# Gate products of a transformer block: seven products for 11 of 32 weight pairs, and new distances of x1's transposes

## The chip, the core and the metric

The kernel runs on one core of a Trainium2 chip, in one launch. The metric is the device time of one execution in microseconds (us). The core's engines work at the same time, each through its own queue of instructions in order: PE (TensorE) multiplies matrices and transposes, DVE (VectorE) and ACT (ScalarE) work on elements, POOL (GpSimd) does a few steps and some transfers, SP (SyncE) issues most transfers. An instruction waits until what it reads is there and what it overwrites is no longer needed. PE writes its sums into eight PSUM banks of 128 x 512 fp32.

## What is computed

One block of a transformer on 256 tokens of width 2048, in fp32. A wide product of the input gives the operands of two branches and two gates. Branch a is a gated delta rule over 8 heads, branch b a sparse attention over 8 heads. Each branch is multiplied by its own weights and by the sigmoid of its gate; their sum goes through an output product, a residual sum with a layer norm, and an FFN of width 5632 with a second residual sum and layer norm. The lines that bear on the change:

```python
proj = x @ w_in[l]
(qkv_a, a_in, b_in, z, q_b, k_b, v_b, q_i, k_i, w_i, gate_a, gate_b) = jnp.split(proj, offsets, axis=-1)
...
merged = jax.nn.sigmoid(gate_a) * (o_a @ w_branch_a[l]) + jax.nn.sigmoid(gate_b) * (o_b @ w_branch_b[l])
x = layer_norm(DEEPNORM_ALPHA * x + merged @ w_out[l], ln1_g[l], ln1_b[l])

h_gate, h_up = jnp.split(x @ w_ffn_in[l], 2, axis=-1)
x = layer_norm(DEEPNORM_ALPHA * x + (jax.nn.silu(h_gate) * h_up) @ w_ffn_out[l], ln2_g[l], ln2_b[l])
```

Each gate is a product of 256 x 2048 with 2048 x 2048.

## The kernel before

Every fp32 operand is split into two parts of a shorter type (fp32r): `hi` is a cast on ACT, `lo` is the rest, a subtraction on DVE. A product is three matmuls into one bank: hi by hi, hi by lo, lo by hi. The input's parts are `XH` and `XL` (four tiles `X_0_85` to `X_3_88` in the profile and its order, hi and lo under one name); 256 tokens are two blocks of 128, `tb` 0 and 1.

Weights stream from HBM in chunks of 512 KB, 128 x 1024. `chunk` (L75 to 79) issues the load into `raw` on SP, the cast to `hi` on ACT (L77) and the subtraction to `lo` on DVE (L79), 70 places ahead of their turn; `raw`, `hi` and `lo` have a few buffers each, so how far this runs ahead of PE is set by PE's giving `hi` free, four chunks back.

PE's and SP's orders are written by hand, in the order of the program text. ACT's and DVE's come from priorities: a step of a chunk counts as 70 places earlier than it stands. After each chunk the code calls `tick()`; it counts a clock and lets the waiting chains (generators that were put in with `start`) issue their next step. A chain says how many ticks, or which event, it waits for, so that the attention, the delta rule and the layer norms are laced into the stream of matmuls. `need` only asserts that an event has been.

The gates: `gate(dst)` runs four blocks of 512 columns. `block_xs` takes two banks from `acc` (one for each `tb`) and goes through eight chunks; a chunk holds two k tiles of 128 rows by 512 columns, and `xs_mm` (L159 to 161) makes 12 matmuls of 512 columns from it. The sigmoid is taken from the bank by ACT. A gate has 384 matmuls. First comes gate b (`gb`, in `s_vT` and `s_t`), then the product of branch b with its weights, multiplied into `gb` (L833), then gate a (`ga`, in `s_kT` and `s_qT`), and branch a's product (L842, L843). During gate a the delta rule's output is gated (L765), transposed on PE into `aux` (L772) and split into `oh` and `ol` (L192, L193).

The FFN's output product already has pairs by seven products: a pair is two k tiles by 1024 columns, 24 matmuls in the plain way. With the scheme of Strassen and Winograd it takes seven block products in place of eight, 21 matmuls, on sums of weight blocks (`wt`, L1045 to 1049, split into `thi` and `tlo`, L1036 and L1038) and on combinations of the activations. Four of the seven products go to four banks of their own (`wbank`), which all such pairs of a group share, and which are combined once per group. `WQ` lists which pairs these are: 11 and 8 of 22.

x1's transposes: after the first residual sum, `ln` normalises each token block in four parts of 512 columns (L890, then L895) on DVE. `x1T_chain` puts PE's transposes of these parts (L808) between the last chunks of the output product and the first of the FFN; `X1T_WAIT = (4, 5)` are the ticks until the first, and `1 + tb` those between them. A tick there stands for six matmuls of 512 columns.

Of the kernel before, what the change touches and what calls it, by code (L numbers as in the profile page):

```python
# [34 lines left out]
X1T_WAIT = (4, 5)  # L35
# [14 lines left out]
def block_kernel(ctx: ExitStack, tc: tile.TileContext, xT, x, cpack, onehot, relb, convw, alog, dtb, gnw,  # L50
                 ws, wws, win, wba, wbb, wo, wfi, wfg, wfo, ln1g, ln1b, ln2g, ln2b, out):
# [944 lines left out]


    def pair_chunks(g, q, pool=None):
        return [chunk(wfo[g, 2 * q + i], pool) for i in range(2)]

    def mm3(o, xh, xl, hi, lo, first, last):
        nc.tensor.matmul(o, xh, hi, start=first, stop=False)  # L1002
        nc.tensor.matmul(o, xh, lo, start=False, stop=False)  # L1003
        nc.tensor.matmul(o, xl, hi, start=False, stop=last)  # L1004

    def plain(bank, cks, q, j, n, tb):

        k = 2 * q + (j + n) % 2
        ts = slice(tb * P, tb * P + P)
        hi, lo = cks[j]  # L1010
        cs = slice(n * 512, (n + 1) * 512)
        mm3(bank[2 * tb + n], hh_[:, k, ts], hl_[:, k, ts], hi[:, cs], lo[:, cs],
            q == 0 and j == 0, q == FT // 2 - 1 and j == 1)

    def plain_pair(bank, g, q):
        cks = pair_chunks(g, q)
        for j in range(2):
            for n in range(2):
                for tb in range(NTB):
                    plain(bank, cks, q, j, n, tb)  # L1020
            tick()

    def seven_pair(bank, wbank, g, q):
# [2 lines left out]
        with tc.high_priority(offset=LEAD):
            ra = wq.tile([P, 1024], F32, name="wraw", tag="wraw")
            nc.sync.dma_start(ra, wfo[g, 2 * q])
            rb = wp.tile([P, 1024], F32, name="raw", tag="raw")
            nc.sync.dma_start(rb, wfo[g, 2 * q + 1])  # L1030
            nc.sync.dma_start(gt.rearrange("p a b t -> p (a b t)").bitcast(F32), d_g[WALL.index(q)])

            def parts(src, tag, pool, bufs):
                n = src.shape[1]
                hi = pool.tile([P, n], F32R, name=tag + "hi", tag=tag + "hi", bufs=bufs)
                nc.scalar.copy(hi, src)  # L1036
                lo = pool.tile([P, n], F32R, name=tag + "lo", tag=tag + "lo", bufs=bufs)
                nc.vector.tensor_sub(lo, src, hi.bitcast(F32))  # L1038
                return [(hi[:, i:i + 512], lo[:, i:i + 512]) for i in range(0, n, 512)]

            b11, b22 = parts(ra, "", wp, None)
            b21, = parts(rb[:, :512], "", wp, None)
            b12 = rb[:, 512:]
            t13 = wq.tile([P, 1024], F32, name="wt", tag="wt")
            nc.vector.tensor_tensor(t13.rearrange("p (a n) -> p a n", a=2), ra.rearrange("p (a n) -> p a n", a=2),  # L1045
                                    bc(b12[:, None, :], [P, 2, 512]), op=OP.add)
            t24 = wq.tile([P, 1024], F32, name="wt", tag="wt")
            nc.vector.tensor_add(t24[:, :512], t13[:, :512], ra[:, 512:])
            nc.vector.tensor_add(t24[:, 512:], t24[:, :512], rb[:, :512])  # L1049
            t1, t3 = parts(t13, "t", wq, 3)  # L1050
            t2, t4 = parts(t24, "t", wq, 3)
        ka, kb = 2 * q, 2 * q + 1
        t0, t1s = slice(0, P), slice(P, S)
        first, last = q == WQ[g][0], q == WQ[g][-1]
        mm3(wbank[0], hh_[:, ka, t0], hl_[:, ka, t0], *b11, first, last)
        mm3(bank[1], gt[:, 0, 3], gt[:, 1, 3], *b22, False, False)
        mm3(bank[0], hh_[:, kb, t0], hl_[:, kb, t0], *b21, False, False)
        tick()
        mm3(wbank[3], gt[:, 0, 0], gt[:, 1, 0], *t1, first, last)
        mm3(wbank[2], gt[:, 0, 2], gt[:, 1, 2], *t3, first, last)  # L1060
        mm3(wbank[1], gt[:, 0, 1], gt[:, 1, 1], *t2, first, last)
        mm3(bank[2], hh_[:, kb, t1s], hl_[:, kb, t1s], *t4, False, False)
        tick()
# [37 lines left out]
    def group(g, ps_std, ps_w, n):  # L1101
        bank = [ps_std() for _ in range(4)]
        wbank = [ps_w() for _ in range(4)]
        for q in range(n):
            if g and q in LN2_LOAD:
                ln2_load(LN2_LOAD.index(q))
            if q in WQ[g]:
                seven_pair(bank, wbank, g, q)
# [4 lines left out]
        return bank
# [154 lines left out]
```

## Time and profile before

| | us |
|---|---|
| three runs | 1496.25, 1495.33, 1495.77 |
| median | 1495.77 |
| profiled execution | 1495.64 |
| its span in the trace | 1493.7 |
| gate b on PE | 406.2 to 493.2 |
| branch b's product | 493.2 to 536.7 |
| gate a on PE | 536.7 to 625.6 |
| branch a's product | 625.6 to 672.0 |

The span is the time from the first to the last instruction in the trace; 1.94 us of the execution lie around it. Times in rows of the trace count from its start. A row of the timeline gives start, duration, engine, line, operation, output and inputs, shape and count; in square brackets the idle time of the engine before it. A row of the groups gives the count, then the busy time and the mean in ns of one, then the idle time ahead of them and what ended it. Durations of matmuls overlap: a matmul of 512 columns shows as 0.39 us, so distances of starts are what counts.

### The profile page before, as it was taken

What the parts mean: (1) busy time and instruction counts of PE and PEld (TensorE: products, weight loads), DVE (VectorE), ACT (ScalarE), POOL (GpSimd) and SP (SyncE); (2) the same over time, 40 slices, a digit from 0 to 9 for tenths busy, and PEclk for the clock granted to TensorE, in tenths of its full rate; (3) what the DMA queues carried; (4) which work ended last, traced back from release to release, by engine and by line L of the source; (5) the groups of instructions that cost most, each with busy time, mean ns of one, the idle gap of its engine ahead of it and who ended that gap; (6) DMA issues with size and microseconds to landing.
All of it is one profiled execution on the core that took longest, in us unless ns stands there. A gap on an engine that the chain in (4) does not pass through costs nothing.

```text
span 1493.7 us, 20700 instructions
## 1 busy us (share of the span) xinstructions
PE 1478.3 (99%) x7863; PEld 1264.3 (85%) x7863; DVE 1010.2 (68%) x1434; ACT 734.4 (49%) x971; POOL 50.4 (3%) x59
## 2 busy tenths in 40 slices
PE   9999999999999999999999999999999999999997
PEld 9888888888888888888878888888888888888885
DVE  5798985466464554475675666666666666999986
ACT  5765443445444444444444545545455455554651
POOL 0011010020010000000000000000000000000000
PEclk9999999999999999999999999999999999999999
DMA  8646574434455655558636666666666566786862
GB/s 290 197 155 195 180 200 143 156 128 169 164 190 195 196 185 191 192 182 297 237 113 197 205 219 211 210 213 216 207 214 217 189 218 222 282 276 236 326 221 91
DMA packets 91828, 303.49 MB, mean 203 GB/s; under 512 B 16385, under 2 KB 17449, under 8 KB 91217
## 3 DMA queue, kind: packets, MB, share of 16 engines
q1 hardware_dynamic: 80592, 283.36, 56.6%
q0 software_dynamic: 4096, 16.45, 3.3%
q10 hardware_dynamic: 7040, 2.36, 0.7%
q8 instruction: 62, 1.02, 0.3%
q14 instruction: 38, 0.30, 0.1%
HBM read 290.40 MB, written 11.73 MB: 202 GB/s over the span
## 4 chain that ended last, share of the span: by engine, by line
PE 97%; DMA 1%; DVE 1%; ACT 0%; issue 0%; SPq 0%; POOLq 0%; DVEq 0%; ACTq 0%
PE acc L139 31%; PE acc L142 15%; PE acc L161 10%; PE acc L160 10%; PE acc L159 10%; PE acc L1003 3%; PE acc L1002 3%; PE acc L1004 3%; PE aux L1003 2%; PE aux L1002 2%; PE aux L1004 2%; DMA raw<-in_win_dram 1%; PE aux L593 1%; PE aux L808 0%; PE aux L747 0%; PE aux L487 0%
## 5 line engine op out<-in xcount | busy, mean ns | idle before, releaser
L79 DVE TENSOR_TENSOR lo<-raw,hi 128x1024 fp32r<-128x1024 f32 (+1 forms) x477 | 585.0, 1230 | 401.4 <-ACT hi L77 400.1
L77 ACT CAST hi<-raw 128x1024 fp32r<-128x1024 f32 (+1 forms) x477 | 496.8, 1044 | 572.9 <-PE acc L161 225.9
L139 PE MATMUL acc<-X,hi 128*128 128x512 f32 x1984 | 625.8, 397 | 0.0
L142 PEld LDWEIGHTS acc<-X,lo 128*128 128x128 f32 x1984 | 372.7, 188 | 88.0
L142 PE MATMUL acc<-X,lo 128*128 128x256 f32 x1984 | 390.0, 278 | 0.0
L139 PEld LDWEIGHTS acc<-X,hi 128*128 128x128 f32 x1984 | 302.1, 189 | 2.1 <-ACT hi L77 0.7
L159 PE MATMUL acc<-hi,X 128*128 128x512 f32 x544 | 214.3, 394 | 0.0
L161 PE MATMUL acc<-hi,X 128*128 128x512 f32 x544 | 211.9, 390 | 0.0
L160 PE MATMUL acc<-lo,X 128*128 128x512 f32 x544 | 211.8, 389 | 0.0
L161 PEld LDWEIGHTS acc<-hi,X 128*128 128x128 f32 x544 | 102.1, 188 | 21.3
L160 PEld LDWEIGHTS acc<-lo,X 128*128 128x128 f32 x544 | 102.2, 188 | 20.6
L159 PEld LDWEIGHTS acc<-hi,X 128*128 128x128 f32 x544 | 102.2, 188 | 20.4
L1036 ACT CAST thi<-wt 128x1024 fp32r<-128x1024 f32 x38 | 40.0, 1053 | 40.4 <-DVE wt L1049 22.4
L1002 PE MATMUL acc<-hi,hH 128*128 128x512 f32 x131 | 51.0, 389 | 0.0
L1003 PE MATMUL acc<-lo,hH 128*128 128x512 f32 x131 | 51.0, 389 | 0.0
L1004 PE MATMUL acc<-hi,hL 128*128 128x512 f32 x131 | 51.0, 389 | 0.0
L159 PE MATMUL acc<-hi,oh__104 128*128 128x512 f32 x128 | 50.4, 394 | 0.0
L161 PE MATMUL acc<-hi,ol__105 128*128 128x512 f32 x128 | 49.9, 390 | 0.0
L160 PE MATMUL acc<-lo,oh__104 128*128 128x512 f32 x128 | 49.8, 389 | 0.0
L1038 DVE TENSOR_TENSOR tlo<-wt,thi 128x1024 fp32r<-128x1024 f32 x38 | 45.9, 1220 | 2.7 <-ACT thi L1036 2.3
L1002 PE MATMUL aux<-hi,hH 128*128 128x512 f32 x107 | 41.6, 389 | 0.0
L1003 PE MATMUL aux<-lo,hH 128*128 128x512 f32 x107 | 41.6, 389 | 0.0
(346 smaller groups left out, 1393.3 us busy)
## 6 DMA issues: line engine op xcount, KB each, us to landing
raw<-in_wfg_dram SPq DMA_DIRECT2D x168, 512.0 KB, 3.4
raw<-in_win_dram SPq DMA_DIRECT2D x101, 512.0 KB, 4.2
raw<-in_wws_dram SPq DMA_DIRECT2D x80, 512.0 KB, 3.5
raw<-in_wfo_dram SPq DMA_DIRECT2D x69, 512.0 KB, 4.2
raw<-in_wo_dram SPq DMA_DIRECT2D x32, 512.0 KB, 3.3
wraw<-in_wfo_dram SPq DMA_DIRECT2D x19, 512.0 KB, 4.6
gt<-d_g SPq DMA_DIRECT2D x19, 512.0 KB, 6.4
d_g<-gs POOLq DMA_DIRECT2D x17, 512.0 KB, 4.0
```

The costliest lines, as they stand in the source:

```text
L77: nc.scalar.copy(hi, raw)
L79: nc.vector.tensor_sub(lo, raw, hi.bitcast(F32))
L139: nc.tensor.matmul(pss[c], hv[:, kk, cs[c]], X2[k // 4][:, k % 4], start=(k == 0), stop=False, skip_group_check=True)
L142: nc.tensor.matmul(pss[c][:, :S], lv[:, kk, cs[c]], xh[:, k, :], start=False, stop=(k == KT - 1), skip_group_check=True)
L159: nc.tensor.matmul(ps, xh, hv[:, kk], start=(k == 0), stop=False)
L160: nc.tensor.matmul(ps, xh, lv[:, kk], start=False, stop=False)
L161: nc.tensor.matmul(ps, xl, hv[:, kk], start=False, stop=(k == 2 * n - 1))
L1002: nc.tensor.matmul(o, xh, hi, start=first, stop=False)
L1003: nc.tensor.matmul(o, xh, lo, start=False, stop=False)
L1004: nc.tensor.matmul(o, xl, hi, start=False, stop=last)
L1036: nc.scalar.copy(hi, src)
L1038: nc.vector.tensor_sub(lo, src, hi.bitcast(F32))
```

## The change

Each gate's columns are taken as two groups of 1024 in place of four blocks of 512, and `gate_group` runs eight pairs of k tiles in each: plain ones of 24 matmuls, or by seven products, 21 matmuls, where `GQ` names the pair. `GQ` names 2 of 8 in the first group and 3 of 8 in each of the others, 11 of 32 together. The functions of the FFN's output product are made general (`mm3`, `plain`, `plain_pair`, `seven_pair`, with the line numbers L200 to 270) and serve both; the FFN's instructions and their order stay as they were. The gate weights come from an array of their own, `wgt`, laid out in pairs; there are as many loads of 512 KB as before.

A group holds four banks, from `acc` and `aux` in turn, and the shared products of its seven-product pairs take four more from the other pool. `gate_chain` brings these to SBUF and combines them; at the end of the group they are added to the banks on DVE and the sigmoid is taken from SBUF. The sums of weights and their parts (`g_wraw`, `g_wt`, `g_thi`, `g_tlo`, two buffers each) lie in tiles of the attention and the delta rule that are no longer used, and so do the combinations of x (`g_form`), which `forms_chain` makes for pairs 4, 6 and 2 once, and all four groups use.

On PE, the place is inside a gate, at the start of a pair. Before, where the k tiles of `X_2_87` follow those of `X_1_86`:

```order
L159 MATMUL acc<-hi,X_1_86 128x512
L160 MATMUL acc<-lo,X_1_86 128x512
L161 MATMUL acc<-hi,X_1_86 128x512
L159 MATMUL acc<-hi,X_2_87 128x512
L160 MATMUL acc<-lo,X_2_87 128x512
L161 MATMUL acc<-hi,X_2_87 128x512
```

Now, at pair 4 of the first group, the first by seven products (`g_form` are the combinations of x, `g_thi` and `g_tlo` the parts of the sums of weights, `aux` the shared banks):

```order
L202 MATMUL aux<-hi,X_2_87 128x512
L203 MATMUL aux<-lo,X_2_87 128x512
L204 MATMUL aux<-hi,X_2_87 128x512
L202 MATMUL acc<-hi,g_form_3940 128x512
L203 MATMUL acc<-lo,g_form_3940 128x512
L204 MATMUL acc<-hi,g_form_3940 128x512
L202 MATMUL acc<-hi,X_2_87 128x512
L203 MATMUL acc<-lo,X_2_87 128x512
L204 MATMUL acc<-hi,X_2_87 128x512
L202 MATMUL aux<-g_thi,g_form_3940 128x512
L203 MATMUL aux<-g_tlo,g_form_3940 128x512
L204 MATMUL aux<-g_thi,g_form_3940 128x512
```

Here the pair has seven blocks of three matmuls where a plain one has eight; the shared banks come in at its first block, and the sums of weights at its fourth.

On DVE, the place is the start of gate a, behind the last instructions of branch b's product (`s_vT` and `s_t` are gate b). Before:

```order
L833 TENSOR_TENSOR s_vT<-acc,s_vT 128x512
L833 TENSOR_TENSOR s_t<-acc,s_t 128x512
L79 TENSOR_TENSOR lo<-raw,hi 128x1024 x4
L193 TENSOR_TENSOR ol__105<-aux,oh__104 128x4x128 x2
L79 TENSOR_TENSOR lo<-raw,hi 128x1024
L193 TENSOR_TENSOR ol__105<-aux,oh__104 128x4x128 x2
```

Now, from the third row behind that product on:

```order
L236 TENSOR_TENSOR g_tlo<-g_wt,g_thi 128x1024
L236 TENSOR_TENSOR lo<-g_wraw,hi 128x1024
L250 TENSOR_TENSOR g_wt<-g_wt,raw 128x512
L236 TENSOR_TENSOR lo<-raw,hi 128x512
L246 TENSOR_TENSOR g_wt<-g_wraw,raw 128x1024
L236 TENSOR_TENSOR g_tlo<-g_wt,g_thi 128x1024
L249 TENSOR_TENSOR g_wt<-g_wt,g_wraw 128x512
L80 TENSOR_TENSOR lo<-raw,hi 128x1024
L194 TENSOR_TENSOR ol__105<-aux,oh__104 128x4x128 x2
L250 TENSOR_TENSOR g_wt<-g_wt,raw 128x512
L80 TENSOR_TENSOR lo<-raw,hi 128x1024
L194 TENSOR_TENSOR ol__105<-aux,oh__104 128x4x128 x2
```

Before, only splits of chunks stand there and the two pairs of `ol` splits. Now sums of weights and their parts (L246, L249, L250, and L236 on `g_tlo`) for pair 2 stand ahead of the first `ol` splits, and one more sum ahead of the second.

Also on DVE, around x1's transposes (`x_0` and `x_1` are the two token blocks; `X_0_85` to `X_3_88` here are the splits of the transposes, whose turn follows PE's). Before:

```order
L890 SCALAR_TENSOR_TENSOR x_0_5988<-x_0_5988,mv,lng 128x512
L79 TENSOR_TENSOR lo<-raw,hi 128x1024
L193 TENSOR_TENSOR X_0_85<-aux,X_0_85 128x4x128
L895 SCALAR_TENSOR_TENSOR x_0_5988<-x_0_5988,rs,lnb 128x512
L193 TENSOR_TENSOR X_1_86<-aux,X_1_86 128x4x128
L79 TENSOR_TENSOR lo<-raw,hi 128x1024 x2
L193 TENSOR_TENSOR X_2_87<-aux,X_2_87 128x4x128
L79 TENSOR_TENSOR lo<-raw,hi 128x1024
L193 TENSOR_TENSOR X_3_88<-aux,X_3_88 128x4x128
L882 SCALAR_TENSOR_TENSOR x_1_5989<-x_1_5989,acc 128x512
```

Now:

```order
L1018 SCALAR_TENSOR_TENSOR x_0_6106<-x_0_6106,mv,lng 128x512
L80 TENSOR_TENSOR lo<-raw,hi 128x1024
L1023 SCALAR_TENSOR_TENSOR x_0_6106<-x_0_6106,rs,lnb 128x512
L194 TENSOR_TENSOR X_0_85<-aux,X_0_85 128x4x128
L80 TENSOR_TENSOR lo<-raw,hi 128x1024 x2
L194 TENSOR_TENSOR X_1_86<-aux,X_1_86 128x4x128
L80 TENSOR_TENSOR lo<-raw,hi 128x1024
L194 TENSOR_TENSOR X_2_87<-aux,X_2_87 128x4x128
L1010 SCALAR_TENSOR_TENSOR x_1_6107<-x_1_6107,acc 128x512
L194 TENSOR_TENSOR X_3_88<-aux,X_3_88 128x4x128
```

Token block 0's last L895 (now L1023) now stands ahead of all four splits, two splits of chunks stand ahead of the second, and the first residual sum of token block 1 ahead of the last.

The diff, cut to its core:

```diff
-X1T_WAIT = (4, 5)
+X1T_WAIT = ((5, 1, 1, 1), (6, 1, 2, 2))
...
+GQ = ((4, 6), (2, 4, 6), (2, 4, 6), (2, 4, 6))
...
+    def seven_pair(bank, wbank, src, sh, sl, q, form, home, first, last):
+        with tc.high_priority(offset=LEAD):
+            ra = home("wraw")
+            nc.sync.dma_start(ra, src[2 * q])
+            rb = wp.tile([P, 1024], F32, name="raw", tag="raw")
+            nc.sync.dma_start(rb, src[2 * q + 1])
+            form = form(q)
+            def parts(v, hi, lo):
+                nc.scalar.copy(hi, v)
+                nc.vector.tensor_sub(lo, v, hi.bitcast(F32))
+                return [(hi[:, i:i + 512], lo[:, i:i + 512]) for i in range(0, v.shape[1], 512)]
+            def chunk_parts(v):
+                n = v.shape[1]
+                return parts(v, *(wp.tile([P, n], F32R, name=t, tag=t) for t in ("hi", "lo")))
+            b11, b22 = chunk_parts(ra)
+            b21, = chunk_parts(rb[:, :512])
+            t13 = home("wt")
+            nc.vector.tensor_tensor(t13.rearrange("p (a n) -> p a n", a=2), ra.rearrange("p (a n) -> p a n", a=2),
+                                    bc(rb[:, None, 512:], [P, 2, 512]), op=OP.add)
+            t24 = home("wt")
+            nc.vector.tensor_add(t24[:, :512], t13[:, :512], ra[:, 512:])
+            nc.vector.tensor_add(t24[:, 512:], t24[:, :512], rb[:, :512])
+            t1, t3 = parts(t13, home("thi"), home("tlo"))
+            t2, t4 = parts(t24, home("thi"), home("tlo"))
+        ka, kb = 2 * q, 2 * q + 1
+        t0, t1s = slice(0, P), slice(P, S)
+        mm3(wbank[0], sh[:, ka, t0], sl[:, ka, t0], *b11, first, last)
+        mm3(bank[1], *form(3), *b22, False, False)
+        mm3(bank[0], sh[:, kb, t0], sl[:, kb, t0], *b21, False, False)
+        tick()
+        mm3(wbank[3], *form(0), *t1, first, last)
+        mm3(wbank[2], *form(2), *t3, first, last)
+        mm3(wbank[1], *form(1), *t2, first, last)
+        mm3(bank[2], sh[:, kb, t1s], sl[:, kb, t1s], *t4, False, False)
+        tick()
+    def forms(g, a1, a2, b1, b2):
+        nc.vector.tensor_sub(g[:, 0], a2, b2)
+        nc.vector.tensor_sub(g[:, 1], a1, g[:, 0])
+        nc.vector.tensor_sub(g[:, 2], a2, a1)
+        nc.vector.tensor_sub(g[:, 3], b1, g[:, 1])
...
+    gates_home, gates_form = {}, {}
+    def gates_buffers():
+        for tag, dtype, old in (("wraw", F32, "s_e"), ("wt", F32, "s_bm"), ("thi", F32R, "s_in"), ("tlo", F32R, "s_u")):
+            gates_home[tag] = [0, T("g_" + tag, [P, 2, 1024], dtype, tag=old)]
+        for q, old in ((4, "s_ak"), (6, "s_sq")):
+            t = T(f"g_form{q}", [P, 2, 4, P], F32R, tag=old)
+            gates_form[q] = t[:, 0], t[:, 1]
+        gates_form[2] = [p1.tile([P, 4, P], F32R, name="g_form2", tag="rel", bufs=2) for _ in range(2)]
+    def home(tag):
+        e = gates_home[tag]
+        e[0] += 1
+        return e[1][:, e[0] % 2]
+    def forms_chain(room):
+        for q in (4, 6, 2):
+            yield 1
+            x32 = room[:, :512].rearrange("p (k t) -> p k t", k=2)
+            g = room[:, 512:].rearrange("p (i t) -> p i t", i=4)
+            ks = slice(2 * q % 4, 2 * q % 4 + 2)
+            nc.vector.tensor_add(x32, XH[q // 2][:, ks].bitcast(F32), XL[q // 2][:, ks].bitcast(F32))
+            forms(g, x32[:, 0, :P], x32[:, 0, P:], x32[:, 1, :P], x32[:, 1, P:])
+            split(*gates_form[q], g)
+    def gate_chain(v, wbank):
+        p1_, n6, n7, n5 = wbank
+        nc.scalar.copy(v[0], p1_)
+        nc.scalar.copy(v[2], n6)
+        nc.vector.tensor_sub(v[2], v[2], p1_)
+        nc.vector.tensor_add(v[1], n5, v[2])
+        yield 1
+        nc.vector.tensor_add(v[2], v[2], n7)
+        nc.vector.tensor_add(v[3], n5, v[2])
+    def gate_group(dst, i):
+        c0 = i % 2 * 1024
+        v = [dst[tb][:, c0 + n * 512:c0 + n * 512 + 512] for tb in range(NTB) for n in range(2)]
+        std, shared = (ps_aux, ps_acc) if i % 2 else (ps_acc, ps_aux)
+        bank = [std() for _ in range(4)]
+        for q in range(KT // 2):
+            if q in GQ[i]:
+                if q == GQ[i][0]:
+                    wbank = [shared() for _ in range(4)]
+                seven_pair(bank, wbank, wgt[i], xh, xl, q, lambda q: lambda f: [t[:, f] for t in gates_form[q]], home,
+                           q == GQ[i][0], q == GQ[i][-1])
+                if q == GQ[i][-1]:
+                    start(gate_chain(v, wbank))
+            else:
+                plain_pair(bank, wgt[i], xh, xl, q, q == KT // 2 - 1)
         for j in range(4):
-            for tb, ps in enumerate(block_xs(w_in_block(), xh, xl)):
-                nc.scalar.activation(dst[tb][:, j * 512:(j + 1) * 512], ps, AF.Sigmoid)
+            nc.vector.tensor_tensor(v[j], bank[j], v[j], op=OP.subtract if j == 2 else OP.add)
+            nc.scalar.activation(v[j], v[j], AF.Sigmoid)
...
-    need("lg")
-    gate(gb)
-    need("ob")
+    need("lg", "ob", "o", "mask")
+    gates_buffers()
+    start(forms_chain(gb[1][:, 1024:]))
+    for i in range(2):
+        gate_group(gb, i)
     for j in range(4):
         js = slice(j * 512, (j + 1) * 512)
         for tb, ps in enumerate(block_xs([wbb[j, k] for k in range(4)], oh_, ol_)):
             nc.vector.tensor_mul(gb[tb][:, js], ps, gb[tb][:, js])
     event("bb")
-    need("o")
-    gate(ga)
+    for i in range(2):
+        gate_group(ga, 2 + i)
     need("oa")
...
     def x1T_chain(tb):
-        yield X1T_WAIT[tb]
         for j in range(4):
+            yield X1T_WAIT[tb][j]
             with tc.high_priority(offset=3 * LEAD):
                 transposed_split(x1, j, tb)
-            yield 1 + tb
...
+        "wgt": paired(np.concatenate([w[:, o["gb"]:o["gb"] + 2048], w[:, o["ga"]:o["ga"] + 2048]], axis=1)),
```

More of the change, by code (lines that the diff above doesn't have):

```diff
@@ L196, in bc, with mm3, pair_chunks, plain @@
         return ap.to_broadcast(shape)
+    def mm3(o, sh, sl, hi, lo, first, last):
+        nc.tensor.matmul(o, sh, hi, start=first, stop=False)
+        nc.tensor.matmul(o, sh, lo, start=False, stop=False)
+        nc.tensor.matmul(o, sl, hi, start=False, stop=last)
+    def pair_chunks(src, q, pool=None):
+        return [chunk(src[2 * q + j], pool) for j in range(2)]
+    def plain(bank, cks, sh, sl, q, j, n, tb, last):
+        k = 2 * q + (j + n) % 2
+        ts = slice(tb * P, tb * P + P)
+        hi, lo = cks[j]
+        cs = slice(n * 512, (n + 1) * 512)
+        mm3(bank[2 * tb + n], sh[:, k, ts], sl[:, k, ts], hi[:, cs], lo[:, cs], q == 0 and j == 0, last and j == 1)
@@ new lines, in plain_pair @@
+    def plain_pair(bank, src, sh, sl, q, last):
+        cks = pair_chunks(src, q)
+        for j in range(2):
+            for n in range(2):
+                for tb in range(NTB):
+                    plain(bank, cks, sh, sl, q, j, n, tb, last)
+            tick()
[33 more added lines that the diff above has]
+        mm3(bank[2], sh[:, kb, t1s], sl[:, kb, t1s], *t4, False, False)
+        tick()
@@ L994, in block_kernel @@
     mp_ = fh.enter_context(tc.tile_pool(name="mp", bufs=1, side="right", reuse_waits="tile"))
[L998 to L1023, printed above, removed]
-        gt = wq.tile([P, 2, 4, P], F32R, name="gt", tag="gt", bufs=3)
[L1026 to L1063, printed above, removed]
@@ L1065, in out_block, with streamed, wq_home @@
+    def streamed(q):
+        gt = wq.tile([P, 2, 4, P], F32R, name="gt", tag="gt", bufs=3)
+        nc.sync.dma_start(gt.rearrange("p a b t -> p (a b t)").bitcast(F32), d_g[WALL.index(q)])
+        return lambda i: (gt[:, 0, i], gt[:, 1, i])
+    def wq_home(tag):
+        return wq.tile([P, 1024], F32R if tag in ("thi", "tlo") else F32, name=tag, tag=tag,
+                       bufs=3 if tag in ("thi", "tlo") else 2)
     def out_block(tb, g, n):
@@ L1111, in group @@
             else:
-                plain_pair(bank, g, q)
+                plain_pair(bank, wfo[g], hh_, hl_, q, q == FT // 2 - 1)
         return bank
@@ L1132, in block_kernel @@
     for q in range(FT // 2 - HELD, FT // 2):
-        cks = pair_chunks(1, q, ex2 if q < FT // 2 - HELD // 2 else None)
+        cks = pair_chunks(wfo[1], q, ex2 if q < FT // 2 - HELD // 2 else None)
         for j in range(2):
             for n in range(2):
-                plain(bank, cks, q, j, n, 0)
+                plain(bank, cks, hh_, hl_, q, j, n, 0, q == FT // 2 - 1)
             tick()
@@ L1158, in block_kernel @@
             for j in range(2):
-                plain(bank, cks, q, j, n, 1)
+                plain(bank, cks, hh_, hl_, q, j, n, 1, q == FT // 2 - 1)
         add_out(1, 1, n, bank[2 + n])
```

21 lines of the change are left out of this document (9 added, 12 removed).

## The prediction

> **What bounds the kernel now.** I read the page's totals and its chain of waits first, then the waits of PE, then the four stretches of time that the change touches.
>
> ```profile
> PE 1478.3 (99%) x7863; PEld 1264.3 (85%) x7863; DVE 1010.2 (68%) x1434; ACT 734.4 (49%) x971; POOL 50.4 (3%) x59
> PEclk9999999999999999999999999999999999999999
> PE 97%; DMA 1%; DVE 1%; ACT 0%; issue 0%; SPq 0%; POOLq 0%; DVEq 0%; ACTq 0%
> PE acc L125 <- DVE lo L79: 1.5, 3, 0.8
> PE aux L808 <- issue: 1.3, 2, 1.0
> PE aux L294 <- DVE s_bm L291: 1.3, 1, 1.3
> ```
>
> PE is busy 99% of the span at the full granted clock, and 97% of the chain that ended last is PE. The waits name nothing in the gates; the only ones in reach of the change are the two, 1.3 us together, of x1's transposes (L808). By stretches:
>
> ```profile
> core 0: us, PE busy (x) PEld busy (x) DVE busy (x) ACT busy (x) POOL busy (x), PEclk, DMA share, GB/s
> 406.00:493.00 87.00, 87.00 (x386) 72.03 (x385) 46.47 (x48) 42.24 (x43) 4.63 (x1) 1.00 0.59 193
> 537.00:625.00 88.00, 88.00 (x398) 73.02 (x397) 41.94 (x38) 39.46 (x43) 0.00 (x0) 1.00 0.57 190
> 755.00:782.00 27.00, 25.70 (x130) 20.76 (x129) 22.68 (x33) 11.10 (x15) 1.00 (x1) 1.00 0.45 153
> 1256.00:1368.00 112.00, 112.00 (x496) 92.72 (x495) 104.04 (x112) 64.05 (x71) 0.00 (x0) 1.00 0.72 250
> ```
>
> They are gb's gate, ga's gate, x1's transposes, and the first half of the FFN's output product, where 11 of 22 weight pairs already go by seven products. In both gates PE has no gap, while DVE is idle for nearly half. A busy PE need not be one at its peak, so what a matmul is worth is read from starts:
>
> ```profile
> 419.77 0.39 PE L159 MATMUL acc<-hi,X 128*128 128x512 f32 x1
> ...
> 430.88 0.39 PE L160 MATMUL acc<-lo,X 128*128 128x512 f32 x1
> ```
>
> Between these starts lie 49 steps: 11.11 / 49 = **0.2267 us** each, with a weight load in every step. The FFN's output product shows what leaving matmuls out brings:
>
> ```profile
> 1266.79 0.39 PE L1002 MATMUL acc<-hi,hH 128*128 128x512 f32 x1
> ...
> 1271.55 0.39 PE L1002 MATMUL aux<-hi,hH 128*128 128x512 f32 x1
> ...
> 1276.99 0.39 PE L1002 MATMUL acc<-hi,hH 128*128 128x512 f32 x1
> ```
>
> The first stretch is a pair of 21 matmuls, 4.76 us; the second is one of 24, 5.44 us. The difference, 0.68 us, is three steps of 0.2267. So a pair by seven products is cheaper by just what it leaves out, as long as PE is fed.
>
> **The change, part by part.**
>
> *Matmuls.* 11 pairs lose 3 matmuls of 512 columns each: 33 x 0.2267 = **7.48 us**. Nothing covers this: PE is the path in both gates.
>
> *Feeding DVE.* I price a pair by what the FFN's output product takes there:
>
> ```profile
> L79 DVE TENSOR_TENSOR lo<-raw,hi 128x1024 fp32r<-128x1024 f32 x22 | 26.5, 1221 | 4.5 <-ACT hi L77 4.4
> L1038 DVE TENSOR_TENSOR tlo<-wt,thi 128x1024 fp32r<-128x1024 f32 x22 | 26.7, 1220 | 0.3
> L1038 DVE TENSOR_TENSOR lo<-wraw,hi 128x1024 fp32r<-128x1024 f32 x11 | 13.4, 1219 | 0.7 <-ACT hi L1036 0.5
> L1045 DVE TENSOR_TENSOR wt<-wraw,raw 128x1024 f32<-128x1024 f32 x11 | 13.4, 1218 | 0.9 <-DMA raw<-in_wfo_dram 0.9
> L1038 DVE TENSOR_TENSOR lo<-raw,hi 128x512 fp32r<-128x512 f32 x11 | 7.5, 684 | 0.0
> L1049 DVE TENSOR_TENSOR wt<-wt,raw 128x512 f32<-128x512 f32 x11 | 7.6, 688 | 0.2
> 1289.21 1.22 DVE L79 TENSOR_TENSOR lo<-raw,hi 128x1024 fp32r<-128x1024 f32 x1
> 1290.35 1.22 DVE L1038 TENSOR_TENSOR lo<-wraw,hi 128x1024 fp32r<-128x1024 f32 x1
> 1291.48 0.69 DVE L1038 TENSOR_TENSOR lo<-raw,hi 128x512 fp32r<-128x512 f32 x1
> 1292.08 0.69 DVE L1048 TENSOR_TENSOR wt<-wt,wraw 128x512 f32<-128x512 f32 x1
> ```
>
> The last four rows are starts: queued one behind the other, 1024 columns cost 1.14 us and 512 cost 0.60, a little less than their durations. A seven-product pair has four instructions of 1024 (three splits, one sum) and three of 512: 4 x 1.14 + 3 x 0.60 = 6.36 us of DVE (6.94 by durations), against 4.76 us of PE. A plain pair has two: 2.28 (2.44) against 5.44. A group of 1024 columns with three such pairs, five plain ones and eight more instructions of 512 (the shared sums and the sum ahead of the sigmoid) takes 3 x 6.36 + 5 x 2.28 + 8 x 0.60 = 35.3 us of DVE (38.5 by durations, with 0.69 for the eight), and 183 x 0.2267 = 41.5 us of PE. ACT takes 3.5 casts instead of 2 per such pair and two copies per group, at 1.05 us per 1024 columns under 30 us of 41.5. The FFN stretch is denser (DVE 104.04 of 112 us) and PE there never waited. The cost is nothing, PE's matmuls hide it; without that cover it is the slower rival below. SP issues as many loads of 512 KB, in as many ticks.
>
> *Forms.* The four combinations of x for three pairs (19 instructions of DVE and 3 casts, 6 to 7 us in all) go among the attention's:
>
> ```profile
> 349.19 2.19 DVE L724 TENSOR_SCALAR s_bm<-s_bm,sume 128x256 f32<-128x256 f32 x8
> 355.45 1.04 PE L732 MATMUL aux<-ident,s_bm 128*128 128x128 f32 x8
> ```
>
> The softmax ends at 351.38 and its transposes come at 355.45, so there are 4.1 us of room; about 2.2 us of the forms stand ahead of that row. Cost nothing; at worst PE would wait a microsecond here.
>
> *Joins.* The shared sums take four PSUM banks that the transposes and the next group use as well. The tightest place I found is the start of ga's first group, where the transposes of `oh`'s second half end:
>
> ```profile
> 549.33 0.48 PE L159 MATMUL acc<-hi,X 128*128 128x512 f32 x1
> 550.96 1.28 DVE L193 TENSOR_TENSOR ol__105<-aux,oh__104 128x512 fp32r<-128x512 f32 x2
> ```
>
> 549.33 is the first matmul behind them; the two `ol` splits, which free their banks, ended at 551.60 and 552.24. In the new order PE wants these banks 12 and 15 matmuls behind the transposes: 549.33 + 2.72 = 552.05 and 552.73, half a microsecond after each split. One sum of 512 columns more stands ahead of the splits on DVE (0.60 us), where DVE had over a microsecond idle. At the other joins the rows ahead of the needed copy leave 0.6 to 1.2 us by my count, at the first group 0.3. I take nothing for all of them; the other bound is a wait of an operation's length, about 0.9 us, at each of four places: 3.6 us. Less than nothing they can't be, since PE had no gap here.
>
> *x1's transposes.*
>
> ```profile
> 755.72 0.39 PE L161 MATMUL acc<-hi,X 128*128 128x512 f32 x1
> 756.45 0.63 PE L808 MATMUL aux<-ident,x 128*128 128x128 f32 x4 [0.35 <-issue]
> 770.37 0.39 PE L161 MATMUL acc<-hi,X 128*128 128x512 f32 x1
> 771.72 0.63 PE L808 MATMUL aux<-ident,x 128*128 128x128 f32 x4 [0.96 <-issue]
> 754.95 1.41 DVE L895 SCALAR_TENSOR_TENSOR x<-x,rs,lnb 128x512 f32<-128x512 f32 x2
> 770.87 1.41 DVE L895 SCALAR_TENSOR_TENSOR x<-x,rs,lnb 128x512 f32<-128x512 f32 x2
> ```
>
> Measured by starts, PE came at 755.72 + 0.23 = 755.95 and waited 0.50 us; then at 770.60, and waited 1.12: each time for the block of x1 that DVE's L895 wrote (ended 756.36, and at about half of the last row, 771.57). One tick later is six matmuls, 1.36 us. The first wait vanishes. For the second PE now comes at 770.60 - 0.50 + 1.36 = 771.46, and 0.26 is left if DVE's row stands where it was. Gain 0.50 + 0.86 = **1.36 us**; bounds are nothing (something else holds PE by as much) and 1.62 (DVE's row comes sooner too).
>
> *Sum.* The profiled execution took 1495.64 us, 1.94 more than its span of 1493.7, and stands 0.13 below the median 1495.77. 1495.64 - 7.48 - 1.36 = **1486.8 us**.
>
> **The rivals.**
>
> *Late joins.* The four waits of about 0.9 us come in full: 1486.8 + 3.6 = 1490.4. For it speaks how thin the margins are; against it, that the FFN stretch has such joins without a wait.
>
> *A matmul is worth less than its step.* If only the weight load, 0.188 us, went with each matmul, 33 x 0.188 = 6.2 and the time is 1488.1. The stretch 1266.79 to 1276.99 speaks against it. The Trainium skill, "TensorE: Matmul & The Clock Gate", section "Back-to-back issue gap", says that a stream of loads and matmuls sustains about 131 ns per matmul of 512 columns, since both pipeline; by that 4.3 us would go and the time be about 1490.0. The trace disagrees, with 0.2267 over 49 steps.
>
> *PE is not the bound.* Then the matmuls' 7.48 us turn up as waits for loads or splits, and only the transposes count: 1494.3. For it: PEld is busy only 85%, and DMA 0.57 to 0.59 of the gates. The Trainium skill, "Perfetto Trace Analysis", section "Identifying the Most-Contended Engine", says that matmul busy time misjudges the distance from peak and load busy time should be taken. Against it: the constant step, and a stretch with DMA at 0.72 that kept it. The same time would come of a change that does not do what it says.
>
> *DVE sets the pace.* The splits run ahead of PE by four chunks, about 8 us; `g_thi` and `g_tlo` have two buffers each where the FFN's have three. If the lead can't be rebuilt between such pairs, because the second `g_thi` waits for PE and the lo splits behind it on DVE wait with it, each pair costs DVE's time: (6.36 or 6.94) - 4.76 = 1.6 to 2.2 us, x 11 = 18 to 24, against 7.48 saved and 1.36: 1504 to 1510, slower. It decides as soon as each pair costs more than 8.84 / 11 = 0.80 us beyond PE's 4.76. Against it: a plain pair lies between any two, and leaves DVE 5.44 - 2.28 = 3.2 us to catch up, twice what a seven-product pair falls behind.
>
> **How the numbers follow.** Forecast 0.73, its own range 1486.0 to 1488.2 (the transposes' bounds, and the runs' scatter of 0.45 us); late joins 0.14; a matmul worth less 0.04; PE not the bound 0.05; DVE sets the pace 0.04. From the forecast's lower end less a little, 1485.8, to the late joins' 1490.4, the first three lie inside and some 0.15 outside. A difference of 0.2%, 3.0 us, is about what can be told from no change: 1492.8 and 1498.8. The first three cases are faster, 0.91; the fourth is the same, 0.05; the last slower, 0.04.
>
> **What would show it.** Right: 33 matmuls fewer; a plain pair in the gates 5.44 us and a seven-product pair 4.76; no wait of PE at the first shared product of each group nor at the first product after a join; the gates 537 us and 406 us stretches shorter by 4.1 and 3.4 us; the waits at x1's transposes 0 and about 0.3 us. Wrong: waits of PE for `g_tlo` or `lo` inside the groups (DVE sets the pace), for the banks at a join, for `raw` loads, or longer steps between matmuls.

## The result, and the profile after

| | before | after |
|---|---|---|
| median of six runs, us | 1495.72 | 1487.09 |
| lowest to highest, us | 1495.24 to 1496.25 | 1486.29 to 1487.69 |
| ratio, 95% interval | | 0.9942 (0.9932 to 0.9952) |
| profiled execution, us | 1495.64 | 1486.29 |
| its span, us | 1493.7 | 1483.8 |

The change makes the kernel 8.6 us faster; 8.84 us were forecast, and 1486.8 us as the time. The page after the change shows the same picture with less in it (totals, chain, and PE's waits):

```profile
PE 1470.8 (99%) x7830; PEld 1258.6 (85%) x7830; DVE 1079.4 (73%) x1539; ACT 755.7 (51%) x1004; POOL 50.4 (3%) x59
PE 98%; DMA 1%; DVE 1%; SPq 0%; issue 0%; ACT 0%; POOLq 0%; DVEq 0%
PE aux L368 <- DVE s_bm L365: 1.3, 1, 1.3
PE acc L202 <- DVE s_vT L961: 0.3, 1, 0.3
PE acc L126 <- DVE lo L80: 0.2, 1, 0.2
```

There are 33 matmuls fewer, DVE has 69 us more work, and PE is still the chain. The waits of x1's transposes (L808 before, L934 now) are gone from the list. There is one new entry, a wait for L961, at the start of gate a. In the timeline of PE the stages start here:

```profile
404.71 0.39 PE L202 MATMUL acc<-hi,X 128*128 128x512 f32 x1
488.37 0.39 PE L160 MATMUL acc<-hi,oh__104 128*128 128x512 f32 x1
531.89 0.39 PE L202 MATMUL acc<-hi,X 128*128 128x512 f32 x1
617.35 0.39 PE L160 MATMUL acc<-hi,oh__104 128*128 128x512 f32 x1
663.78 0.39 PE L160 MATMUL acc<-hi,X 128*128 128x512 f32 x1
```

These are gate b, branch b's product, gate a, branch a's product, and what follows. Set against the same places of the trace before:

| stretch on PE, us | before | after | difference |
|---|---|---|---|
| up to gate b | 406.17 | 404.71 | -1.46 |
| gate b | 87.04 | 83.66 | -3.38 |
| branch b's product | 43.52 | 43.52 | 0 |
| gate a | 88.86 | 85.46 | -3.40 |
| branch a's product | 46.43 | 46.43 | 0 |
| from there to the last matmul | 810.11 | 808.44 | -1.67 |

The first row belongs to neither part of the change. It differs between executions (405.9, 405.4 and 405.7 us in the first three experiments), and the difference of 1.46 us arises in the first 30 us of the trace, at the first loads and splits. So the span fell by 9.9 us, of which 8.45 us are the change.

### The profile page after: what moved, and what is told of

The parts are those of the page before. It is cut to its first block, busy times and chain, and to the rows that moved or that the text cites. A ratio compares the mean times of both kernels' runs of the same rounds, so it can differ in the third digit from the quotient of the medians.

```text
span 1483.8 us, 20772 instructions
## 1 busy us (share of the span) xinstructions
PE 1470.8 (99%) x7830; PEld 1258.6 (85%) x7830; DVE 1079.4 (73%) x1539; ACT 755.7 (51%) x1004; POOL 50.4 (3%) x59
## 4 chain that ended last, share of the span: by engine, by line
PE 98%; DMA 1%; DVE 1%; SPq 0%; issue 0%; ACT 0%; POOLq 0%; DVEq 0%
PE acc L140 31%; PE acc L143 15%; PE acc L160 6%; PE acc L162 6%; PE acc L161 6%; PE acc L202 5%; PE acc L203 5%; PE acc L204 5%; PE aux L203 4%; PE aux L202 4%; PE aux L204 4%; PE aux L667 1%; PE aux L934 0%; PE acc L126 0%; PE acc L123 0%; PE acc L125 0%
## 5 line engine op out<-in xcount | busy, mean ns | idle before, releaser
L80 DVE TENSOR_TENSOR lo<-raw,hi 128x1024 fp32r<-128x1024 f32 (+1 forms) x455 | 557.4, 1229 | 322.7 <-ACT hi L78 320.1
L78 ACT CAST hi<-raw 128x1024 fp32r<-128x1024 f32 (+1 forms) x455 | 473.0, 1043 | 512.0 <-PE acc L140 206.3
L160 PE MATMUL acc<-hi,X 128*128 128x512 f32 x288 | 114.5, 398 | 0.0
L162 PE MATMUL acc<-hi,X 128*128 128x512 f32 x288 | 112.3, 390 | 0.0
L161 PE MATMUL acc<-lo,X 128*128 128x512 f32 x288 | 112.2, 389 | 0.0
L162 PEld LDWEIGHTS acc<-hi,X 128*128 128x128 f32 x288 | 54.1, 188 | 11.5
L161 PEld LDWEIGHTS acc<-lo,X 128*128 128x128 f32 x288 | 54.2, 188 | 10.4
L160 PEld LDWEIGHTS acc<-hi,X 128*128 128x128 f32 x288 | 54.1, 188 | 10.4
L236 DVE TENSOR_TENSOR tlo<-wt,thi 128x1024 fp32r<-128x1024 f32 x38 | 45.9, 1219 | 2.6 <-ACT thi L235 2.3
```

The source lines that it names most:

```text
L78: nc.scalar.copy(hi, raw)
L80: nc.vector.tensor_sub(lo, raw, hi.bitcast(F32))
L160: nc.tensor.matmul(ps, xh, hv[:, kk], start=(k == 0), stop=False)
L161: nc.tensor.matmul(ps, xh, lv[:, kk], start=False, stop=False)
L162: nc.tensor.matmul(ps, xl, hv[:, kk], start=False, stop=(k == 2 * n - 1))
L236: nc.vector.tensor_sub(lo, v, hi.bitcast(F32))
```

## The experiments

The kernels of one batch ran on one chip with the kernel before, whose median there is given. Shorter differences are read from the traces, by the same stretches as above.

**1. The gates alone.** The changed kernel with the old distances:

```diff
-X1T_WAIT = ((5, 1, 1, 1), (6, 1, 2, 2))
+X1T_WAIT = ((4, 1, 1, 1), (5, 2, 2, 2))
```

> The gate part alone: the changed kernel with x1's transposes at the old distances. My theory: the two waits of PE come back, 0.50 and 1.1 us by the starts of its matmuls, and the time is 1487.1 + 1.6 = 1488.7 us. By the sum as predicted (1.36) it is 1488.4. Rival: the waits are hidden elsewhere and the time stays 1487.1.

Measured 1488.96 us (before 1495.22; ratio 0.9958, 0.9946 to 0.9971). The entry in the waits of PE is back:

```profile
PE aux L934 <- issue: 1.3, 2, 1.0
```

The last stretch takes 810.09 us, as before the change (810.11), and 808.44 with the new distances. So the two waits are worth 1.6 to 1.7 us, as in the first of the two sums expected.

**2. The distances alone**, in the kernel before (`yield X1T_WAIT[tb][j]` ahead of each transpose, with the new numbers).

> The distances alone: the kernel before with x1's transposes at the new distances. My theory: both waits of PE at the transposes fall below 0.1 us and the time is 1495.7 - 1.6 = 1494.1 us. As predicted, 0.26 us is left at the second and the time is 1494.4. Rival: 1495.7, nothing gained, PE waits elsewhere.

Measured 1493.86 us (before 1495.22; ratio 0.9992, 0.9984 to 1.0001). The medians differ by 1.36 us, which the interval can't tell from nothing. The trace tells it: the last stretch takes 808.44 us instead of 810.11, and both waits are gone:

```profile
756.27 0.39 PE L161 MATMUL acc<-hi,X 128*128 128x512 f32 x1
756.50 0.60 PE L808 MATMUL aux<-ident,x 128*128 128x128 f32 x4
...
770.42 0.39 PE L161 MATMUL acc<-hi,X 128*128 128x512 f32 x1
770.67 0.63 PE L808 MATMUL aux<-ident,x 128*128 128x128 f32 x4
```

The transposes of the first token block start 0.23 us after the matmul ahead of them, those of the second 0.25: one step of 0.23 and no wait.

**3. Four pairs in place of eleven.**

```diff
-GQ = ((4, 6), (2, 4, 6), (2, 4, 6), (2, 4, 6))
+GQ = ((4,), (4,), (4,), (4,))
```

> One pair by seven products in each group (pair 4), 4 in place of 11, all else as in the changed kernel. My theory: each pair that is plain again costs three steps, 7 x 0.68 = 4.76 us; the first sum of weights of gate a's first group moves two pairs later, so PE's wait of 0.55 us at the start of gate a is gone too: 1487.1 + 4.8 - 0.5 = 1491.3 us, with steps of 0.2267 us throughout the gates. Rival, a matmul is worth its load of 0.188 us: 1487.1 + 3.9 - 0.5 = 1490.5, with longer steps in the seven-product pairs than in the plain ones. Rival, PE is not the bound: 1487 with the time in waits.

Measured 1491.13 us (before 1495.22; ratio 0.9972, 0.9961 to 0.9983). Gate b takes 85.68 us and gate a 87.50, each 1.36 us less than before the change: two pairs at 0.68. PE waits nowhere in the gates. A pair is worth three whole steps, not three loads.

**4. More pairs, with two buffers.** `GQ = ((4, 6), (2, 3, 4, 6), (2, 3, 4, 6), (2, 3, 4, 6))`, pair 3 with pair 4's combinations of x.

> Four of eight pairs by seven products in three groups (pairs 2, 3, 4, 6; pair 3 takes the combinations of x of pair 4, so its products are not the reference's), 14 in place of 11. DVE per group: by spacing 4 x 6.36 + 4 x 2.28 + 4.8 = 39.4 us, by durations 43.0, against PE's 180 x 0.2267 = 40.8. My theory: by spacing PE still sets the pace, 1487.1 - 3 x 0.68 = 1485.1 us, with PE's waits for lo or g_tlo below 1 us in all. Rival, DVE sets the pace by durations: 1485.1 + 3 x 2.2 = 1491.7 us, with waits of PE for lo or g_tlo in three groups; or, with two buffers of g_thi and adjacent pairs, each adjacent pair costs DVE's 6.4 in place of 4.8: 1485.1 + 6 x 1.6 = 1494.7.

Measured 1494.36 us (before 1495.22; ratio 0.9996, 0.9987 to 1.0005). Three pairs more, and of the gain of 8.6 us only 0.9 is left, which the interval can't tell from nothing:

```profile
PE acc L203 <- DVE g_tlo L236: 3.7, 3, 1.5
PE aux L203 <- DVE g_tlo L236: 1.5, 1, 1.5
```

PE waits for `g_tlo` four times; three of these are 1.73 to 1.78 us by the starts, each at the third of three pairs side by side, and the fourth, at a second pair, is 0.87. So the expectation that went by DVE's mean load, less than 1 us of waits in all, was wrong. The time is near the rival on adjacent pairs, 1494.7, but in part by luck: that sum has 1.6 us at each of six adjacent pairs, 9.6 us, while in the trace the waits for `g_tlo` make up 6.1 us, two stretches at about half the clock behind them (see the last section) some 3.2, and the wait at the start of gate a (experiment 7) 0.95. Whether the two buffers or DVE's load bring the waits about, this run can't tell.

**5 and 6. Is it the load or the buffers?** Eleven pairs as in the changed kernel, but side by side, with one pair's combinations of x for all; then the same with a third buffer.

```diff
-GQ = ((4, 6), (2, 4, 6), (2, 4, 6), (2, 4, 6))
+GQ = ((4, 6), (4, 5, 6), (4, 5, 6), (4, 5, 6))
...
+        for tag, old in (("thi", "s_ak"), ("tlo", "s_sq")):
+            gates_home[tag][1].append(T("g_" + tag + "3", [P, 1024], F32R, tag=old))
```

(The last two lines are in the second kernel only; the tiles that they take held combinations of x.)

> As many pairs by seven products as in the changed kernel (11, three in a group), but side by side: pairs 4, 5, 6 in three groups. Only one pair's combinations of x are made and used for all, so the products are not the reference's. DVE's work per group is as in the changed kernel. Theory that DVE's average sets the pace: no waits for lo or g_tlo, and with the first such pair of gate a two pairs later its wait of 0.55 us is gone, 1486.6 us. My theory from the run with four pairs per group: the third pair side by side finds both g_thi buffers taken, DVE's queue stands and its lead is lost; PE waits 2 to 4 us in each of three groups, 1493 to 1499 us.

> The same with a third buffer each for g_thi and g_tlo (in the two tiles that held combinations of x). If the two buffers are what loses the lead, the waits for g_tlo fall to less than half of those of the same kernel with two, and the time is 1487 to 1490 us. If it is DVE's own 6.4 us per pair against PE's 4.8, three pairs side by side lose 3 x 1.6 = 4.8 us of a lead of about 6 and the waits vanish only if the lead was whole at the start; if they stay as with two buffers, the buffers are not the cause.

With two buffers 1494.01 us (before 1494.82; ratio 0.9992, 0.9983 to 1.0001), with three 1486.39 (0.9943, 0.9928 to 0.9958). The work is the same. With two, gates b and a take 87.55 and 89.30 us; with three, 83.77 and 84.94. With two, PE waits three times for `g_tlo`, once in each group of three such pairs, by 1.74 to 1.75 us; that is less than the 2 to 4 us expected, and a stretch at about half the clock behind one of the waits costs another 1.6. With three it waits nowhere in the gates, and the time is a little below the 1487 to 1490 us expected. The timelines of ACT show why. First with two buffers, then with three, at the cast of the third sum in gate a's first group:

```profile
562.56 0.62 ACT L235 CAST hi<-raw 128x512 fp32r<-128x512 f32 x1
563.65 1.05 ACT L235 CAST g_thi<-g_wt 128x1024 fp32r<-128x1024 f32 x1 [0.47 <-PE aux L204]
565.02 1.06 ACT L235 CAST g_thi<-g_wt 128x1024 fp32r<-128x1024 f32 x1 [0.31 <-PE acc L204]
```

```profile
553.84 1.05 ACT L235 CAST hi<-g_wraw 128x1024 fp32r<-128x1024 f32 x1 [2.10 <-PE acc L204]
554.80 1.05 ACT L235 CAST g_thi<-g_wt 128x1024 fp32r<-128x1024 f32 x1
556.56 0.62 ACT L235 CAST hi<-raw 128x512 fp32r<-128x512 f32 x1 [0.71 <-ACT g_thi L235]
```

With three the cast at 554.80 is made right behind a cast of `hi`, 22.1 us after gate a's first matmul (at 532.73 in that run); with two, the one at 563.65 has waited until PE was done with the first buffer, 27.2 us after it (536.45 in its run). DVE then has the splits of `g_tlo` all at once:

```profile
569.41 0.68 DVE L249 TENSOR_TENSOR g_wt<-g_wt,g_wraw 128x512 f32<-128x512 f32 x1
570.01 1.22 DVE L236 TENSOR_TENSOR g_tlo<-g_wt,g_thi 128x1024 fp32r<-128x1024 f32 x1
571.15 0.68 DVE L250 TENSOR_TENSOR g_wt<-g_wt,raw 128x512 f32<-128x512 f32 x1
571.75 2.35 DVE L80 TENSOR_TENSOR lo<-raw,hi 128x1024 fp32r<-128x1024 f32 x2
574.02 1.22 DVE L236 TENSOR_TENSOR g_tlo<-g_wt,g_thi 128x1024 fp32r<-128x1024 f32 x1
```

These are the rows with two buffers: one without a gap behind the other, and PE, which wanted the last at 573.5, went on at 575.29. So the lead is lost by the buffer, and side by side it can't be made up. In the changed kernel the plain pair between two gives the buffer back in time. The slack, from the end of a `g_tlo` on DVE to PE's first matmul with it, says the same: it is 1.99 us or more in the changed kernel; at the last `g_tlo` of the third pair side by side it is 0.05 us with two buffers, where PE stands waiting, and 1.2 to 1.4 us with three. So three buffers leave little for a fourth pair.

**7. The wait at the start of gate a.** In the changed kernel PE's third block of gate a waits. The rows of DVE, then of PE:

```profile
530.67 1.22 DVE L246 TENSOR_TENSOR g_wt<-g_wraw,raw 128x1024 f32<-128x1024 f32 x1 [1.71 <-DMA raw<-in_wgt_dram]
531.81 1.22 DVE L80 TENSOR_TENSOR lo<-raw,hi 128x1024 fp32r<-128x1024 f32 x1
532.95 0.68 DVE L961 TENSOR_TENSOR s_vT<-acc,s_vT 128x512 f32<-128x512 f32 x1
533.02 0.39 PE L204 MATMUL acc<-hi,X 128*128 128x512 f32 x1
533.69 0.50 PE L202 MATMUL acc<-hi,X 128*128 128x512 f32 x1 [0.27 <-DVE s_vT L961]
```

Branch b's product ends at 531.89; its last two banks are read by L961, which stands behind a sum of weights and a split. PE wants the first of them two blocks later, at 533.25, and gets it at 533.69; the next step is 0.11 us longer. That is 0.55 us. It differs between executions: in experiment 1, whose gates are the same, this place costs 0.80 us, and gate a takes 85.71. The experiment takes the first pair of gate a bank by bank:

```diff
-        for j in range(2):
-            for n in range(2):
+        for a in range(2):
+            for b in range(2):
+                j, n = (b, a) if by_bank else (a, b)
```

> The changed kernel with the first pair of gate a taken bank by bank (both chunks for columns 0 to 511, then for 512 to 1023), so that PE wants the last two banks of branch b's product 2.72 us after it in place of 1.36. My theory: DVE frees them 1.76 and 2.36 us after it, behind the sum of weights and a split; the wait of 0.55 us at the start of gate a is gone, gate a takes 84.9 in place of 85.5 us, 1486.5 us. Rival: the chunk that is now wanted 1.36 us sooner is late, and PE waits for lo there by as much.

Measured 1486.51 us (before 1494.82; ratio 0.9944, 0.9932 to 0.9957). PE's list of waits has none in the gates any more (one step, at the first `g_tlo` of gate a, is still 0.11 us longer), and gate a takes 84.98 us. The medians can't tell the half microsecond from the changed kernel's, the trace does.

**8 and 9. A twelfth pair.** The same, with `GQ = ((2, 4, 6),) * 4`; and that without POOL's multiplication of `s_rv`.

> The same, with pair 2 of the first group also by seven products, 12 in all; the products are the reference's. My theory: another 0.68 us, 1485.8 us, gate b 83.0 in place of 83.7 us. Rival: the shared banks, wanted two pairs sooner, are not free at the start of the first group, and PE waits there by 0.5 us or more.

> The version with 12 pairs, with POOL's multiplication of s_rv by the norm's weights (4.62 us at the start of gate b) left out, so the output of branch a lacks these weights. If DVE's split of 4.82 us beside it (1.14 us elsewhere) took the lead of which PE's wait of 0.73 us at pair 2 of the first group was short: no split over 1.3 us there, the wait is gone, gate b takes 83.0 in place of 83.9 us and the time is about 1485.9 us. If DVE's other work at this place (sums for pair 2 and the gating of branch a's output) is the cause, the wait stays within 0.3 us of 0.73.

The first measured 1486.67 us (before 1494.82; ratio 0.9943, 0.9931 to 0.9956): gate b takes 83.93 us, and PE waits 0.73 us for `g_tlo` behind its matmul of 430.34; gate a takes 85.23, 0.25 more than in experiment 7, most of it at its first pair by seven products. So the pair brings nothing. It was not the banks, which the rival had named. DVE and POOL at the start of gate b in this kernel:

```profile
408.54 0.69 DVE L251 TENSOR_TENSOR g_wt<-g_wt,raw 128x512 f32<-128x512 f32 x1
411.78 4.82 DVE L237 TENSOR_TENSOR lo<-g_wraw,hi 128x1024 fp32r<-128x1024 f32 x1 [2.56 <-ACT hi L236]
416.52 0.68 DVE L237 TENSOR_TENSOR lo<-raw,hi 128x512 fp32r<-128x512 f32 x1
410.89 4.62 POOL L836 TENSOR_TENSOR s_rv<-s_rv,gnw 128x2048 f32<-128x2048 f32 x1 [83.09 <-ACT s_rv L835]
```

A split of 1024 columns, 1.22 us elsewhere, takes 4.82 while POOL multiplies. Without POOL's row the same split reads:

```profile
412.06 1.22 DVE L237 TENSOR_TENSOR lo<-g_wraw,hi 128x1024 fp32r<-128x1024 f32 x1
```

The wait is gone, gate b takes 83.01 us, and the time is 1486.12 (before 1495.31; ratio 0.9941, 0.9923 to 0.9958). The step at POOL's cost is shown; a version that keeps the multiplication and avoids the collision was not tried.

**10 and 11. How far does it go with three buffers?** Five pairs side by side (2 to 6) in three groups, one pair's combinations of x for all; and a version with the reference's products and 14 pairs (`GQ = ((4, 5, 6), (4, 5, 6), (3, 4, 5, 6), (3, 4, 5, 6))`).

> Three buffers each for g_thi and g_tlo, the first pair of gate a bank by bank, and five pairs side by side in three groups (2 to 6; 17 in all). One pair's combinations of x are used for all, so the products are not the reference's. DVE's work in such a group is 5 x 6.36 + 3 x 2.28 + 4.8 = 43.4 us by spacing against PE's 177 x 0.2267 = 40.1. If PE still sets the pace (the lead covers it): 1487.1 - 0.5 - 6 x 0.68 = 1482.5 us with no waits for lo or g_tlo. If DVE sets the pace: five pairs lose 5 x 1.6 = 8.0 us of a lead of about 6, PE waits some 2 to 3 us for g_tlo in each of three groups, 1488 to 1492 us.

> A version with the reference's products: three buffers each for g_thi and g_tlo, the first pair of gate a bank by bank, pairs 4, 5, 6 in gate b's groups and 3, 4, 5, 6 in gate a's, 14 in all; the combinations of x lie in other tiles no longer used, those of pair 3 are made at the start of gate a. If PE sets the pace: 1487.1 - 0.5 - 3 x 0.68 = 1484.6 us, gate b 82.4 us and gate a 83.6. Rival: four pairs side by side lose 6.4 us, the whole lead, and PE waits up to a microsecond for g_tlo in each of gate a's groups: 1485.5 to 1486.6.

Five measured 1501.94 us (before 1495.82; ratio 1.0039, 1.0024 to 1.0054), slower than before the change, and 10 us above the 1488 to 1492 that were expected if DVE sets the pace. PE waits 9.0 us in all for `g_tlo`, and 3.0 us for the `ol` splits at the start of gate a:

```profile
PE acc L203 <- DVE g_tlo L237: 7.0, 7, 1.4
PE aux L202 <- DVE ol__105 L194: 3.0, 2, 2.3
PE aux L203 <- DVE g_tlo L237: 2.0, 2, 1.4
```

The windows of its second and last group:

```profile
core 0: us, PE busy (x) PEld busy (x) DVE busy (x) ACT busy (x) POOL busy (x), PEclk, DMA share, GB/s
446.00:488.00 42.00, 39.30 (x159) 30.22 (x157) 39.17 (x45) 27.19 (x32) 0.00 (x0) 0.96 0.49 177
574.00:629.00 55.00, 49.43 (x209) 38.50 (x208) 53.52 (x59) 33.77 (x40) 0.00 (x0) 1.00 0.54 190
```

In the second row DVE is busy 97% and PE 90%: here DVE sets the pace. The 14 pairs measured 1491.25 us (before 1495.82; ratio 0.997, 0.9959 to 0.9981), 4 us slower than the changed kernel by the ratios, and 4.6 us above the upper end of what was expected (1486.6):

```profile
PE aux L204 <- DVE g_tlo L238: 2.7, 3, 1.2
PE aux L203 <- DVE s_t L927: 1.2, 1, 1.2
```

Most of that is in gate b (87.71 us), where three pairs side by side meet DVE's other work, and DVE reaches the banks of the first group's join too late for the second group (L927). Gate a, with four pairs, takes 85.70, 2.3 us more than 88.86 less eight times 0.68.

## Why the prediction was right, and where it was off

*Matmuls, forecast 7.48 us.* Right in size and place: gate b gave 3.38 of 3.40 us forecast for its five pairs, experiment 3 gave 1.36 us for each two pairs, and the first such pair of gate b starts at 426.46 and the pair behind it at 431.23, 4.77 us on. Gate a gave 3.40 of 4.08; of the 0.68 that is missing, 0.55 is the wait under *Joins*, and the rest lies in some thirty steps of 0.229 to 0.236 us. So 6.8 us of 7.48 came. The rival of a matmul worth only its load is out, and so is that of PE not being the bound.

*Feeding DVE at no cost.* Right for this spacing, with reserve: 74.57 us busy in the 85 us from 532 to 617 of gate a is 88%, inside the 85 to 93% of the two estimates (with gate a's other work on DVE counted in), and no wait for a split. But the reason given was incomplete. The rival *DVE sets the pace* had named the two buffers, yet what was held against it was DVE's time alone, with the plain pair in between as time to catch up; experiments 5 and 6 show that the plain pair's first service is to give `g_thi` back. With the same load side by side 7.6 us are lost, and a third buffer brings them back.

*Joins, forecast nothing, bound 3.6 us.* The place named as tightest, the `ol` splits at gate a's first shared products, held here (with five pairs side by side, experiment 10, PE did wait there). The wait came some 14 us sooner at the same start: L961 behind a sum of weights that the change had put there. The prediction's account of "the other joins" left 0.6 to 1.2 us and missed that this one has two blocks of matmuls, 1.36 us, until PE wants a bank, against 1.74 us until DVE has released it (531.89 to 533.63). It cost 0.55 us; experiment 7 takes it away. Of the four late joins of the rival, of about 0.9 us each, this is the only one that came.

*x1's transposes, forecast 1.36 us.* Mis-sized by the term that was named: the 0.26 us left at the second wait did not stay, since DVE's row did not stand where it was. Counted from the end of branch a's product it starts 98.60 us after it (762.38 less 663.78), 0.25 us sooner than before (770.87 less 672.02, 98.85). It is 98.61 us in experiment 2, and 98.85 again in experiment 1, with the old distances. So the new distances bring it; by which step on DVE was not followed.

```profile
762.99 0.39 PE L162 MATMUL acc<-hi,X 128*128 128x512 f32 x1
763.23 0.63 PE L934 MATMUL aux<-ident,x 128*128 128x128 f32 x4
762.38 0.74 DVE L1023 SCALAR_TENSOR_TENSOR x<-x,rs,lnb 128x512 f32<-128x512 f32 x1
```

DVE's row ends at 763.12 and PE's transposes start at 763.23, one step after the matmul ahead of them. The gain is the upper bound, 1.6 us, as experiments 1 and 2 show each by itself. Gate a gained 0.7 us less than forecast and the transposes 0.3 us more. That these partly cancel is luck; what is left between the 1487.09 measured and the 1486.8 forecast is within the scatter of the runs.

*DVE sets the pace, given 0.04.* The mechanism is real, and close. At the spacing of the change it does not bite; three pairs more (experiment 4) took back nearly the whole gain, and six more with three buffers made the kernel slower than before. Its price was set at 1.6 to 2.2 us per pair; the long waits of experiment 4 are 1.7 to 1.8 us each, but only at every third pair. With two buffers it is the wait for `g_thi` that the rival had described which costs the lead (experiments 5 and 6); that DVE's own load does it too shows only in experiment 10.

*The forms* in the attention chain cost nothing: no new wait of PE stands there. (They are 18 instructions of DVE, not 19.)

## What to carry to other kernels

On a bound PE whose steps are constant, a matmul left out is worth its whole step, as long as the engines that feed it keep their lead. Whether they do is not decided by their mean load alone: count, for each buffer, when the bound engine gives it back, since one buffer too few makes the feeding engines late even where they have time to spare. And at each join look at what the scheduler puts ahead of the instruction that frees a bank; the row that matters may be one that the change moved there for a later pair.

## What the runs showed of the hardware

A wait of PE can cost more than its length. In experiment 4, behind a wait of 1.77 us, some eight matmuls run at about half the clock (0.51 is granted in their window). The rows of PE, then its windows around them (with the granted clock in the third column):

```profile
564.45 0.50 PE L203 MATMUL aux<-g_tlo,g_form 128*128 128x512 f32 x1 [1.49 <-DVE g_tlo L236]
...
566.38 0.63 PE L203 MATMUL acc<-lo,X 128*128 128x512 f32 x1
566.80 0.63 PE L204 MATMUL acc<-hi,X 128*128 128x512 f32 x1
```

```profile
core 0: us, PE busy (x), PEclk, DMA share, GB/s
559.00:562.40 3.40, 3.40 (x15) 1.00 0.59 182
562.40:565.50 3.10, 1.55 (x5) 0.99 0.90 264
565.50:568.90 3.40, 3.40 (x10) 0.51 0.24 66
568.90:572.00 3.10, 3.10 (x15) 1.00 0.39 145
```

Seven steps take 0.427 us in place of 0.227, and the steps beside them a part of that more: 1.6 us on top of the wait. Of the six waits of 1.73 to 1.78 us in experiments 4 and 5, three were followed by such a stretch and three were not. The length of the wait alone does not decide it: in experiment 10 one of 2.50 us was followed by steps of full rate, and one of 1.49 us by such a stretch. What does decide it, these traces do not show. It also widens the scatter: of the eleven runs of experiment 4, the five shortest (1491.74 to 1493.95 us) have a mean granted clock of 0.998, and the four longest (1495.82 to 1497.44 us) one of 0.995. The Trainium skill, "TensorE: Matmul & The Clock Gate", section "Why this matters for your kernels", tells to avoid gaps of over some 3 us for this reason; the half rate agrees with these traces, but here a wait of under 2 us was enough.

The other is the split on DVE that took 4.82 us beside POOL's multiplication of 4.62 us (experiments 8 and 9), where it takes 1.22 alone. It starts 0.89 us into POOL's row and ends 1.09 us after it: DVE seems to stand still meanwhile. The Trainium skill, "SBUF — State Buffer", section "SBUF: two separate sides", states such a lock between POOL and a DVE operation with two inputs in SBUF, and this case agrees. In the kernel before, two splits took 5.96 us at the same place, and PE didn't wait there.
